# Beta inside the inverse, modulation pages of four k-tiles, edge fill through two page pools, and paired attention scores in a two-layer hybrid backbone

## The chip, the cores and the metric

The kernel runs on one core of one Trainium2 chip. The metric is device time in microseconds (us) of one execution, the median of several. The engines are TensorE (PE; its weight loads are PEld), VectorE (DVE), ScalarE (ACT), GpSimd (POOL) and SyncE (SP), whose queue issues the loads from HBM.

## The reference

Two layers over 256 latent tokens `x` and 256 context tokens, width 1024. Each layer modulates a normed stream with shift, scale and gate from `silu(c)`, runs three mixers and one output projection, and then a gated FFN with a width-3 convolution over positions.

```python
mod_l = split(silu(c) @ ada_w[layer] + ada_b[layer], 6)      # and mod_c from silu(c_ctx)
p = split_cols(modulate(rms_norm(x, g0), mod[0], mod[1]) @ w_in[layer])
# A, differential attention (4 heads): s = q k^T / 8; p = softmax(s)
w = p[:, :, 0] - lam * p[:, :, 1];  o = w @ v                 # rms_norm after it
# B, bidirectional gated linear recurrence (4 heads); it is not changed
# C, gated delta rule (4 heads, chunks of 64, both directions):
tri = eye(c) + where(strict, beta[:, None] * (k @ k.T) * decay, 0)
rhs = concat([v * beta, k * (beta * exp(gc))])
u, w = triangular_solve(tri, rhs)
v_new = u - w @ state
out = (q * exp(gc)) @ state + ((q @ k.T) * decay) @ v_new
state = exp(g_last) * state + (k * exp(g_last - gc)).T @ v_new
x = x + mod[2] * rms_norm(concat(A, B, C) @ w_out[layer], g1)
u = conv3(modulate(rms_norm(x, g2), mod[3], mod[4]) @ w_up) + b
x = x + mod[5] * rms_norm((silu(u_gate) * u_val) @ w_down, g3)
```

## The kernel before

Everything is held transposed: 128 channels on the partitions, the 512 tokens (context, then latent) along the free dimension, so the width of 1024 is eight tiles ("k-tiles"). A dense product splits weight and activation into a rounded part and a remainder and multiplies three pairs (`whi` by high, `wlo` by high, `whi` by low: lines 283 to 285, and 293 to 295 for 512 columns). Weights come as pages of 128x1024 into a ring `raw` (line 260, issued by SP), are rounded on ACT (line 269), and their remainder is taken on DVE or POOL (line 273).

In time: opening and first projections to about 100 us; mixers of layer 0 to about 400; output projection, residual, norm and the first FFN tiles to about 511 (the "layer-0 edge"); FFN of layer 0 to 810; the edge between the layers; mixers of layer 1 from about 912 to 1142; output projection and edge to 1195; FFN of layer 1 to 1345; the end.

Inside a stage, `weave` (line 1067) runs Python generators, each a stream of work (input projections, delta rule `gdn`, recurrence `hgrn`, attention `da`, modulation `ada`), and always takes the next step of the one that has progressed least, weighed by the numbers of `RATE`. A scheduler then orders the instructions for each engine, so an engine's queue differs from the order of the code. Queues run in order: what waits holds what is behind it.

*Modulation.* `ada` (line 309) makes one block of 512 columns of `silu(c) @ ada_w`. Four pages hold two k-tiles of 512 columns each; eight matmuls (line 317) with a 32-column weight, of which two columns are used, add into four groups of 32 partitions, DVE copies the bank to `adas` (line 320), four transposes turn it (line 323), and a DVE reduction (line 325) adds the four groups. Twelve blocks are made in the mixers' weaves (`ADA`), eight more as `fill` beside the edges (`FILL`: six after the mixers of layer 0, two after those of layer 1). Fill pages come from the pool `kq` (two buffers). The opening has its own `ada_unit` (line 330), whose pages hold four k-tiles of 256 columns (line 337), and whose groups are added by matmuls with the two-column constant `sel` (line 343).

*Delta rule.* `gdn` handles two halves (`hf`) of the tokens, two head pairs (`hp`) each. It forms the strictly triangular `N`, with beta multiplied in on POOL (line 658), and inverts it in six levels of doubling blocks: PE multiplies `N` by the inverse so far (`rt`), DVE masks the result (line 704), ACT and DVE transpose, PE multiplies again (`dT`), and DVE subtracts it from the inverse (line 721; line 707 at level 0). Then POOL forms `R` = beta times v (line 727, tile `gF`) and the decayed keys (line 729), and four chunk steps follow.

*Attention.* For each head and query tile `da` (line 1023) makes two score blocks (line 1035), takes their maxima, scales these by -1/8 (line 1039), exponentiates on ACT, scales the first block by its reciprocal sum (line 1047), combines the two (line 1048), and transposes the result (line 1052).

A matmul of 32-bit floats leaves two records in the trace; the dense ones and the transposes leave one.

## Time and profile before

| | |
|---|---|
| median of 3 runs | 1396.82 us (1396.49 to 1397.12) |
| the profiled execution | 1397.04 us, span 1395.3 |
| PE busy | 1298.6 us, 93% |
| PEld busy | 1048.0 us, 75% |
| DVE busy | 892.5 us, 64% |
| ACT busy | 658.9 us, 47% |
| POOL busy | 393.7 us, 28% |

The span is the time from first to last instruction of the profiled execution. A share of busy time is a mean over stages that differ. What a stage could give is read from its own windows and from the waits of the engine that ends it. Matmuls are pipelined, so the duration of a short one overlaps the next; start to start is then the better measure.

### The profile page before, as it was taken

How to read it: one execution, taken by the hardware profiler on the slowest of the kernel's cores; microseconds unless marked ns; L12 is line 12 of the kernel's file. 1: busy time of each engine (PE TensorE's matmuls, PEld its weight loads, DVE VectorE, ACT ScalarE, POOL GpSimd, SP SyncE). 2: the span in 40 equal slices, each digit the busy share in tenths (PEclk: the TensorE clock that was granted, in tenths of full speed). 3: DMA queues.
4: the chain of work that ended last, by engine and by line, in shares of the span. 5: the costliest groups of instructions: out<-in, count | busy, mean ns of one | idle time of the engine just before them, and what ended most of it. 6: DMA issues, size and time to landing. Idle time of an engine off the chain costs nothing.

```text
span 1395.3 us, 26653 instructions
## 1 busy us (share of the span) xinstructions
PE 1298.6 (93%) x10720; PEld 1048.0 (75%) x10720; DVE 892.5 (64%) x1722; ACT 658.9 (47%) x1189; POOL 393.7 (28%) x378
## 2 busy tenths in 40 slices
PE   5999997999989999999999997999989998999996
PEld 2768665666677678888888886997666765999995
DVE  3565657877647876434543559877697665776665
ACT  3364424444465544323432455675253354655553
POOL 1012014201046223201210266221241024655553
PEclk8999998999999999999999999999999999999998
DMA  8612443112335663323233234544221265455552
GB/s 300 211 46 91 167 165 139 32 47 76 107 121 189 207 217 115 104 92 105 91 101 96 82 122 135 173 145 155 95 103 34 106 243 181 139 183 185 189 167 76
DMA packets 56283, 185.96 MB, mean 133 GB/s; under 512 B 6368, under 2 KB 10464, under 8 KB 56160
## 3 DMA queue, kind: packets, MB, share of 16 engines
q1 hardware_dynamic: 56160, 184.27, 39.9%
q8 instruction: 84, 1.38, 0.4%
q14 instruction: 39, 0.32, 0.1%
HBM read 182.14 MB, written 2.10 MB: 132 GB/s over the span
## 4 chain that ended last, share of the span: by engine, by line
PE 74%; DVE 12%; ACT 5%; POOL 4%; issue 2%; DMA 2%; SPq 0%; DVEq 0%; POOLq 0%; ACTq 0%
PE up L284 8%; PE up L283 8%; PE up L285 8%; PE in L293 6%; PE in L294 5%; PE in L295 5%; PE dn L285 4%; PE dn L284 4%; PE dn L283 4%; PE ada L317 2%; DVE wlo L273 2%; PE sc L1035 2%; PE op L284 1%; PE op L283 1%; PE op L285 1%
## 5 line engine op out<-in xcount | busy, mean ns | idle before, releaser
L273 DVE TENSOR_TENSOR wlo<-raw,whi 128x1024 fp32r<-128x1024 f32 (+2 forms) x241 | 299.8, 1245 | 269.1 <-issue 90.4
L269 ACT CAST whi<-raw 128x1024 fp32r<-128x1024 f32 (+1 forms) x244 | 248.9, 1023 | 122.6 <-PE dn L285 99.0
L285 PE MATMUL up<-h,whi 128*128 128x256 f32 (+1 forms) x768 | 248.7, 324 | 1.3 <-DVE h L441 0.7
L283 PE MATMUL up<-h,whi 128*128 128x256 f32 (+1 forms) x768 | 248.3, 324 | 1.2 <-ACT h L438 1.1
L284 PE MATMUL up<-h,wlo 128*128 128x256 f32 (+1 forms) x768 | 248.0, 324 | 0.9 <-DVE wlo L273 0.9
L293 PE MATMUL in<-h,whi 128*128 128x512 f32 (+1 forms) x496 | 184.8, 373 | 2.2 <-DVE kq L481 2.2
L273 POOL TENSOR_TENSOR wlo<-raw,whi 128x256 fp32r<-128x256 f32 (+1 forms) x111 | 127.1, 1145 | 173.2 <-ACT whi L269 76.4
L294 PE MATMUL in<-h,wlo 128*128 128x512 f32 (+1 forms) x496 | 175.5, 354 | 0.0
L295 PE MATMUL in<-h,whi 128*128 128x512 f32 (+1 forms) x496 | 175.3, 354 | 0.0
L283 PEld LDWEIGHTS up<-h,whi 128*128 128x128 f32 x768 | 145.8, 190 | 19.6 <-issue 4.2
L285 PEld LDWEIGHTS up<-h,whi 128*128 128x128 f32 x768 | 145.9, 190 | 16.4 <-issue 1.7
L284 PEld LDWEIGHTS up<-h,wlo 128*128 128x128 f32 x768 | 145.9, 190 | 15.5 <-DVE wlo L273 1.9
L284 PE MATMUL dn<-gT,wlo 128*128 128x256 f32 (+1 forms) x400 | 127.6, 320 | 3.4 <-DVE wlo L273 3.4
L283 PE MATMUL dn<-gT,whi 128*128 128x256 f32 (+1 forms) x400 | 127.7, 320 | 2.7 <-ACT gT L300 2.7
L285 PE MATMUL dn<-gT,whi 128*128 128x256 f32 (+1 forms) x400 | 127.3, 320 | 0.5 <-POOL gT L302 0.5
L1262 POOL TENSOR_TENSOR u<-u 128x512 f32<-128x512 f32 (+1 forms) x44 | 44.4, 1010 | 278.3 <-DVE u L481 257.5
L293 PEld LDWEIGHTS in<-h,whi 128*128 128x128 f32 x496 | 96.2, 194 | 19.8 <-issue 5.4
L294 PEld LDWEIGHTS in<-h,wlo 128*128 128x128 f32 x496 | 96.2, 194 | 12.7 <-issue 3.5
L295 PEld LDWEIGHTS in<-h,whi 128*128 128x128 f32 x496 | 95.9, 193 | 12.3 <-issue 1.3
L477 ACT ACTIVATE u<-up,vec 128x256 f32<-128x256 f32 (+1 forms) x96 | 61.8, 644 | 75.2 <-PE up L285 75.2
L284 PEld LDWEIGHTS dn<-gT,wlo 128*128 128x128 f32 x400 | 76.7, 192 | 9.1 <-DVE wlo L273 4.0
L283 PEld LDWEIGHTS dn<-gT,whi 128*128 128x128 f32 x400 | 76.8, 192 | 8.2 <-ACT gT L300 3.1
(281 smaller groups left out, 2318.2 us busy)
## 6 DMA issues: line engine op xcount, KB each, us to landing
raw<-ada_w SPq DMA_DIRECT2D x96, 512.0 KB, 4.4
raw<-w_up SPq DMA_DIRECT2D x96, 512.0 KB, 3.5
raw<-w_in SPq DMA_DIRECT2D x68, 512.0 KB, 3.6
raw<-w_down SPq DMA_DIRECT2D x32, 512.0 KB, 3.5
raw<-w_out SPq DMA_DIRECT2D x24, 512.0 KB, 3.5
raw<-w_down SPq DMA_DIRECT2D x24, 384.0 KB, 3.1
x<-xT SPq DMA_DIRECT2D x16, 256.0 KB, 6.1
x_spill<-x SPq DMA_DIRECT2D x8, 128.0 KB, 2.0
```

What stands on the lines that cost most here:

```text
L269: nc.scalar.copy(hi[:, :cols], raw[:, :cols])
L273: e.tensor_sub(lo[:, a:b], raw[:, a:b], hi[:, a:b].bitcast(F32))
L283: nc.tensor.matmul(ps, wh[:, k, :], ah, start=first and k == ks[0], stop=False)
L284: nc.tensor.matmul(ps, wl[:, k, :], ah, start=False, stop=False)
L285: nc.tensor.matmul(ps, wh[:, k, :], al, start=False, stop=last and k == ks[-1])
L293: nc.tensor.matmul(ps, wh[:, k, :], ah, start=k == 0, stop=False)
L294: nc.tensor.matmul(ps, wl[:, k, :], ah, start=False, stop=False)
L295: nc.tensor.matmul(ps, wh[:, k, :], al, start=False, stop=k == n - 1)
L317: nc.tensor.matmul(ps[32 * g:32 * g + 32, :], self.cs[:, k, :], w[:, kk, :], start=k < 4, stop=k >= 4, tile_position=(0, 32 * g))
L477: nc.scalar.activation(dst, ps, AF.Identity, scale=w3[1], bias=bias)
L1035: nc.tensor.matmul(ps[:, :128 * nk], q[64 * m:64 * m + 64, a + 128 * qt:a + 128 * qt + 128], k[64 * m:64 * m + 64, :128 * nk], start=True, ...
L1262: self.nc.gpsimd.tensor_mul(us[0][:, lo:], us[0][:, lo:], us[1][:, lo:])
```

## The change

*Modulation pages.* A page now holds four k-tiles of 256 columns; a block is sixteen matmuls in two column halves, chained so that the scheduler keeps their order. Four `sel` matmuls take the place of the transposes and of the reduction. Fill pages are taken from `g` and `kq` in turn; `g` has six buffers, not seven, and the delta rule no longer takes a page for `R`.

*Delta rule.* Beta is folded into the inverse: the inverse starts from beta on the diagonal, `N` carries only a sign, and at level 0 it is multiplied by beta of one token and, transposed, of the other. The masks go: DVE's subtraction becomes a predicated copy that writes only the positions of this level, and ACT copies `rt` out of PSUM. `R` is the plain value, copied by ACT.

*Attention.* The 1/8 is applied as ACT moves q and k out of PSUM; the maximum is negated as it is taken; both score blocks of a query tile are issued as a pair; the scaling of the first block goes to ACT.

```diff
-RATE = ((121, 197, 32, 218, 37, 8), (53, 64, 15, 50, 5, 7))
+RATE = ((118, 137, 32, 147, 37, 8), (53, 64, 15, 65, 5, 7))
...
@@ ada
-            for kc in range(4):
-                w = self.load_raw(self.I["ada_w"][12 * ly + j - 4, kc], 1024, tags[kc % len(tags)]).rearrange("p (k n) -> p k n", k=2)
...
+            prev = []
+            for i in range(4):
+                half, kc = i // 2, i % 2
+                w = self.load_raw(self.I["ada_w"][12 * ly + j - 4, i], 1024, tags[i % len(tags)]).rearrange("p (k n) -> p k n", k=4)
+                for g in range(4):
+                    x = nc.tensor.matmul(ps[32 * g:32 * g + 32, 256 * half:256 * half + 256], self.cs[:, 4 * kc + g, :], w[:, g, :],
+                                         start=kc == 0, stop=kc == 1, tile_position=(0, 32 * g))
+                    prev = [self._dep(x, prev)]
...
-                nc.tensor.transpose(ps2[:, 128 * i:128 * i + 128], st[:, i * 128:(i + 1) * 128], self.C("ident"))
-            sm = self.small("adr", 8)
-            nc.vector.reduce_sum(sm, ps2.rearrange("p (a g s) -> p a s g", a=4, g=4)[:, :, 0:2, :], axis=AX.X)
+                nc.tensor.matmul(ps2[:, 2 * i:2 * i + 2], st[:, 128 * i:128 * i + 128], self.C("sel"), start=True, stop=True)
...
@@ gdn
-                nc.gpsimd.tensor_tensor(ck(X[hp]), ck(X[hp]), b64(hp, "beta"), ALU.mult)
...
-                nc.vector.tensor_tensor(ck(N[hp]), ck(N[hp]), pkv[hp][:, :, 0, :], ALU.mult)
+                nc.vector.scalar_tensor_tensor(ck(N[hp]), ck(N[hp]), -1.0, pkv[hp][:, :, 0, :], ALU.mult, ALU.mult)
...
-                nc.scalar.copy(ck(MT[hp]), self.C("i64").unsqueeze(1).to_broadcast([P, 8, 64]))
+                nc.gpsimd.tensor_tensor(ck(MT[hp]), self.C("i64").unsqueeze(1).to_broadcast([P, 8, 64]), b64(hp, "beta"), ALU.mult)
...
+                def fill(t, src):
...
+                    nc.vector.copy_predicated(out, m.bitcast(U32), v(src))
...
-                        nc.vector.transpose(mtx[hp], N[hp])
-                for hp in HP:
-                    nc.vector.tensor_tensor(ck(rt[hp]), ck(src[hp]), hgm[:, lev, :].unsqueeze(1).to_broadcast([P, 4, 64]), ALU.mult)
+                        b4 = lambda n: G[n][:, 8 * hp + 4 * hf:8 * hp + 4 * hf + 4].unsqueeze(2).to_broadcast([P, 4, 64])
+                        nc.vector.tensor_tensor(ck(rt[hp]), ck(N[hp]), b4("bo"), ALU.mult)
+                        nc.vector.transpose(mtx[hp], rt[hp])
+                        nc.vector.tensor_tensor(ck(mtx[hp]), ck(mtx[hp]), b4("bi"), ALU.mult)
...
+                for hp in HP:
+                    nc.scalar.copy(rt[hp], src[hp])
...
-                    nc.vector.tensor_tensor(joint(MT[hp], 0, 4, 0), joint(MT[hp], 0, 4, 0), nb(ps2[hp][:, 0:256]), ALU.subtract)
+                    fill(MT[hp], ps2[hp][:, 0:256])
...
-                nc.gpsimd.tensor_tensor(s4(R[hp]), two(vtok[hp]), bsc(hp, "beta"), ALU.mult)
+                nc.scalar.copy(vb[hp], tok[hp][:, 256:512])
...
@@ da
+                    qs = (qt,)
+                    ps = [self.bank("a", "sc") for m in range(2)]
...
+                        for m in (1, 0):
...
-                    nc.vector.tensor_scalar(mx, mx, -0.125, None, ALU.mult)
...
+                        nc.vector.reduce_max(mx[m][:, :len(qs)], ps[m][:, :128 * nk], axis=AX.X, negate=True)
...
-                nc.vector.tensor_scalar(e[0], e[0], rc[0], None, ALU.mult)
...
+                nc.scalar.activation(e0, e0, AF.Copy, scale=r0)
...
@@ mixers
-        self.fill = self.ada_gen([(l, j) for l in range(DEPTH) for j in FILL[ly][l]], "g", ("kq",))
+        self.fill = self.ada_gen([(l, j) for l in range(DEPTH) for j in FILL[ly][l]], "g", ("g", "kq"))
```

How this moves instructions, at three places.

SP's queue at the layer-1 edge, before: `raw` pages are loaded from the output projection's, the modulation's and the FFN's weights. The four loads 11969 to 11981 are those of the last modulation block.

```order
L260 DMA raw_11899<-ada_w 128x1024
L260 DMA raw_12029<-w_up 128x1024
L260 DMA raw_12064<-w_up 128x1024
L260 DMA raw_12106<-w_up 128x1024
L260 DMA raw_12141<-w_up 128x1024
L260 DMA raw_12181<-w_up 128x1024
L260 DMA raw_12216<-w_up 128x1024
L260 DMA raw_11969<-ada_w 128x1024
L260 DMA raw_11973<-ada_w 128x1024
L260 DMA raw_11977<-ada_w 128x1024
L260 DMA raw_11981<-ada_w 128x1024
L260 DMA raw_12257<-w_up 128x1024
```

The same place after. The modulation pages 12078 and 12090 (pool `g`) and 12084 and 12096 (pool `kq`) are those of the last block.

```order
L261 DMA raw_12002<-ada_w 128x1024
L261 DMA raw_12008<-ada_w 128x1024
L261 DMA raw_12078<-ada_w 128x1024
L261 DMA raw_12090<-ada_w 128x1024
L261 DMA raw_12144<-w_up 128x1024
L261 DMA raw_12179<-w_up 128x1024
L261 DMA raw_12221<-w_up 128x1024
L261 DMA raw_12256<-w_up 128x1024
L261 DMA raw_12296<-w_up 128x1024
L261 DMA raw_12331<-w_up 128x1024
L261 DMA raw_12084<-ada_w 128x1024
L261 DMA raw_12096<-ada_w 128x1024
```

Two of the last block's four loads have moved ahead of the six `w_up` loads; the other two still stand behind them.

PE's queue at the same edge, before: `ada_11968` is the bank of the last modulation block, `up` are the first FFN matmuls.

```order
L317 MATMUL ada_11968<-raw_11973,cs 32x512 x2
L283 MATMUL up_12036<-h_11576,whi_12031 128x256
L284 MATMUL up_12036<-h_11576,wlo_12032 128x256
L283 MATMUL up_12071<-h_11576,whi_12066 128x256
L284 MATMUL up_12071<-h_11576,wlo_12067 128x256
L283 MATMUL up_12113<-h_11576,whi_12108 128x256
L285 MATMUL up_12036<-h_11576,whi_12031 128x256
L285 MATMUL up_12071<-h_11576,whi_12066 128x256
L317 MATMUL ada_11968<-raw_11977,cs 32x512 x2
L317 MATMUL ada_11968<-raw_11981,cs 32x512 x2
L323 MATMUL ada_2062_11987<-consts,adas_11985 128x128 x4
L283 MATMUL up_12036<-h_11577,whi_12031 128x256
```

The same place after, with `ada_12077` as the last block; `ss` are the column sums of the norm.

```order
L318 MATMUL ada_12077<-raw_12090,cs 32x256
L383 MATMUL ss_12045<-sq_12053,consts 128x256
L383 MATMUL ss_12045<-sq_12056,consts 128x256
L383 MATMUL ss_12045<-sq_12059,consts 128x256
L383 MATMUL ss_12045<-sq_12062,consts 128x256
L383 MATMUL ss_12045<-sq_12065,consts 128x256
L318 MATMUL ada_12077<-raw_12090,cs 32x256 x3
L318 MATMUL ada_12077<-raw_12096,cs 32x256 x4
L284 MATMUL up_12151<-h_11679,whi_12146 128x256
L285 MATMUL up_12151<-h_11679,wlo_12147 128x256
L325 MATMUL ada_2080_12104<-consts,adas_12102 128x2 x4
L284 MATMUL up_12186<-h_11679,whi_12181 128x256
```

The last two page pieces of the block stood behind seven `up` matmuls and now stand in front of the first; the matmuls that add the groups stand behind two.

POOL's queue in the second half of the delta rule of layer 0, before: `gA` (line 658) is the decay times beta, `gF` (line 727) is `R`, `gB` the decayed keys.

```order
L678 COPY sgl_2152<-gB_1985 128x8
L678 COPY sgl_2153<-gB_1986 128x8
L658 TENSOR_TENSOR gA_1983<-gA_1983,sbeta_640 128x512
L727 TENSOR_TENSOR gF_2725<-gB_1985,sbeta_640 128x512
L729 TENSOR_TENSOR gB_1985<-gB_1985,skd_676 128x256
L727 TENSOR_TENSOR gF_2725<-gB_1986,sbeta_640 128x512
L729 TENSOR_TENSOR gB_1985<-gB_1985,skd_676 128x256
L729 TENSOR_TENSOR gB_1986<-gB_1986,skd_676 128x256 x2
L658 TENSOR_TENSOR gA_1984<-gA_1984,sbeta_640 128x512
```

The same place after; `gC` is the start of the inverse.

```order
L685 COPY sgl_2486<-gB_2274 128x8
L687 TENSOR_TENSOR gC_2488<-consts,sbeta_640 128x512
L687 TENSOR_TENSOR gC_2489<-consts,sbeta_640 128x512
L685 COPY sgl_2487<-gB_2275 128x8
L748 TENSOR_TENSOR gB_2274<-gB_2274,skd_676 128x256 x2
L748 TENSOR_TENSOR gB_2275<-gB_2275,skd_676 128x256 x2
```

The multiplications into `gA` and `gF` are gone; two of the same size from a constant have come.

## Rows read from the trace of the kernel before

**Rows 1.** Windows: length, busy us (records) of each engine, granted clock, DMA share, GB/s.

```profile
100.00:400.00 300.00, 276.61 (x3065) 196.37 (x3063) 200.18 (x491) 134.25 (x301) 55.61 (x53) 0.96 0.29 99
207.40:234.10 26.70, 18.38 (x218) 12.25 (x218) 22.24 (x49) 11.03 (x22) 15.59 (x12) 0.92 0.51 178
230.00:244.00 14.00, 10.53 (x119) 7.24 (x121) 9.69 (x34) 9.54 (x21) 0.00 (x0) 0.51 0.13 39
400.00:525.00 125.00, 116.62 (x819) 95.19 (x820) 88.27 (x144) 67.31 (x121) 49.31 (x47) 0.98 0.60 199
950.00:1150.00 200.00, 185.98 (x2344) 133.35 (x2344) 146.75 (x384) 91.18 (x196) 41.38 (x36) 0.97 0.35 122
1038.00:1046.00 8.00, 6.10 (x56) 5.38 (x58) 6.30 (x16) 2.69 (x5) 0.74 (x1) 0.57 0.67 243
1200.00:1345.00 145.00, 145.00 (x1210) 145.00 (x1210) 97.61 (x135) 81.17 (x122) 79.17 (x86) 1.00 0.58 183
```

**Rows 2.** PE's waits from 100 to 400: waiter, releaser, total us, times, longest.

```profile
PE rt L602 <- DVE gC L707: 8.3, 1, 8.3
PE wt L1052 <- DVE em L1048: 5.0, 6, 1.3
```

**Rows 3.** PE's waits from 950 to 1150.

```profile
PE wt L1052 <- DVE em L1048: 6.6, 5, 2.8
PE ada L323 <- DVE adas L320: 2.8, 1, 2.8
```

**Rows 4.** PE's waits from 400 to 525.

```profile
PE ada L317 <- DMA raw<-ada_w: 2.3, 3, 0.9
```

**Rows 5.** Windows of line 317 (modulation matmuls) alone: length, PE (records), PEld, clock.

```profile
100.00:400.00 300.00, 14.71 (x112) 2.95 (x112) 0.96 0.29 99
400.00:525.00 125.00, 20.09 (x80) 2.83 (x80) 0.98 0.60 199
```

**Rows 6.** Timeline of PE: start, us, engine, line, operation, tiles, shape, count.

```profile
54.29 1.07 PE L337 MATMUL ada<-raw,cs 128*32 128x256 f32 x16
...
56.11 0.50 PE L343 MATMUL ada<-consts,adas 128*128 128x2 f32 x4
56.47 0.47 PE L283 MATMUL in<-h,whi 128*128 128x512 f32 x1
...
468.58 0.60 PE L323 MATMUL ada<-consts,adas 128*128 128x128 f32 x4
468.94 0.36 PE L284 MATMUL up<-h,wlo 128*128 128x256 f32 x1
```

**Rows 7.** Timeline at the layer-1 edge, SP's queue and PE (in brackets: idle before, releaser).

```profile
1168.21 10.82 SPq L260 DMA_DIRECT2D raw<-ada_w  x4
...
1180.00 0.40 PE L285 MATMUL up<-h,whi 128*128 128x256 f32 x2
1181.92 3.16 PE L317 MATMUL ada<-raw,cs 128*32 128x512 f32 x8 [1.52 <-DMA raw<-ada_w]
...
1186.62 0.39 PE L283 MATMUL up<-h,whi 128*128 128x256 f32 x1
```

**Rows 8.** Timeline of POOL and DVE around 220 us.

```profile
215.56 3.70 POOL L727 TENSOR_TENSOR gF<-gB,sbeta 128x512 f32<-128x512 f32 x1
...
226.82 1.72 DVE L668 TENSOR_TENSOR gA<-gA 128x256 f32<-128x256 f32 x1 [3.18 <-POOL gA L658]
```

**Rows 9.** Groups: line, engine, operation, tiles, shapes, count; busy us, mean ns; idle before, releaser.

```profile
L704 DVE TENSOR_TENSOR rt<-rt,consts 128x256 f32<-128x256 f32 x40 | 15.1, 410 | 6.2 <-PE rt L602 6.2
...
L917 DVE COPY_PREDICATED Stot<-consts,hs 128x128 f32<-128x128 uint32 (+1 forms) x36 | 13.6, 438 | 1.6 <-PE hs L892 1.6
...
L1047 DVE TENSOR_SCALAR em<-em,ssm 128x512 f32<-128x512 f32 (+1 forms) x24 | 10.5, 436 | 0.4
...
L710 ACT COPY gC<-gC 128x256 f32<-128x256 f32 x20 | 8.2, 410 | 21.5 <-DVE gC L721 15.3 <-DVE mod L326 4.5 <-DVE gC L707 1.1
...
L1039 DVE TENSOR_SCALAR smx<-smx 128x1 f32<-128x1 f32 x48 | 6.9, 145 | 0.4
```

More of the change, by code (lines that the diff above doesn't have):

```diff
@@ L80 @@
 _n = 0
-for _name, _w in (("ident", 128), ("ones", 128), ("sel", 2), ("sel8", 16), ("eps", 1), ("one", 1), ("bones", 128),
+for _name, _w in (("ident", 128), ("ones", 128), ("sel", 2), ("par", 2), ("sel8", 16), ("eps", 1), ("one", 1), ("bones", 128),
                   ("obones", 128), ("perm", 128), ("i64", 64), ("inc2", 128), ("ninc2", 128), ("pstr2", 128),
@@ L311, in ada @@
             ps = self.bank(bank, "ada")
-            for kc in range(4):
-                w = self.load_raw(self.I["ada_w"][12 * ly + j - 4, kc], 1024, tags[kc % len(tags)]).rearrange("p (k n) -> p k n", k=2)
-                for kk in range(2):
-                    k = 2 * kc + kk
-                    g = k % 4
-                    nc.tensor.matmul(ps[32 * g:32 * g + 32, :], self.cs[:, k, :], w[:, kk, :], start=k < 4, stop=k >= 4,
-                                     tile_position=(0, 32 * g))
+            prev = []
[6 more added lines that the diff above has]
+                    prev = [self._dep(x, prev)]
             st = self.tmp("d2", "adas")
@@ L486, in proj_copy, with evac @@
         yield from self.dense_gen(ps[:, lo:], w, hT, lo, NTOK)
-        self.evac(idx, dst[:, lo:], ps[:, lo:])
+        self.evac(idx, dst[:, lo:], ps[:, lo:], 0.125 if idx >= DA_Q else None)
         yield
-    def evac(self, idx, dst, src):
-        if idx % 2:
+    def evac(self, idx, dst, src, scale=None):
+        if scale is not None:
+            self.nc.scalar.activation(dst, src, AF.Copy, scale=scale)
+        elif idx % 2:
             self.nc.scalar.copy(dst, src)
@@ L753, in gdn @@
                     for s, j in enumerate(js):
-                        self.quad((ck(ps[hp])[H[g], s, :], MTv[hp][H[g], j, :], rv[hp][H[g], j, :], True, True) for g in range(2))
+                        self.quad((ck(ps[hp])[H[g], s, :], MTv[hp][H[g], j, :], rv[hp][s][H[g]], True, True) for g in range(2))
                     nc.scalar.copy(pair(U[hp], i), ck(ps[hp][:, 0:128]))
@@ L1031, in da @@
             for qt in range(2):
-                e, rc = [], []
-                for m in range(2):
-                    ps = self.bank("a", "sc")
-                    nc.tensor.matmul(ps[:, :128 * nk], q[64 * m:64 * m + 64, a + 128 * qt:a + 128 * qt + 128],
-                                     k[64 * m:64 * m + 64, :128 * nk], start=True, stop=True)
-                    mx = self.small("mx", 1, 4)
-                    nc.vector.reduce_max(mx, ps[:, :128 * nk], axis=AX.X)
-                    nc.vector.tensor_scalar(mx, mx, -0.125, None, ALU.mult)
-                    em = self.tmp("d2", "em")[:, :128 * nk]
-                    sm = self.small("sm", 1, 4)
-                    self.act(em, ps[:, :128 * nk], AF.Exp, scale=0.125, bias=mx, accum_out=sm)
-                    nc.vector.reciprocal(sm, sm)
-                    e.append(em)
-                    rc.append(sm)
```

65 lines of the change are left out of this document (49 added, 16 removed).

## The prediction

> **What bounds the kernel now.** I read the page first, then TensorE's waits stage by stage, then the stages as windows, then one place in each. In the page PE is busy 1298.6 us of a 1395.3 us span, and the chain that ended last is PE for 74%: TensorE's queue sets the end, and a gain must come off PE's busy time, its idle time or its clock. The windows say where there is room [rows 1]. From 1200 to 1345 us PE is busy all 145 us with 1210 matmul records at clock 1.00, 0.12 us a record: nothing that other engines do matters there. The layer-0 mixers (100 to 400) leave PE idle 23.4 us, the first layer-0 edge (400 to 525) 8.4, the layer-1 mixers (950 to 1150) 14.0. In two short stretches the granted clock reads 0.51 and 0.57, near the lower of its two levels (1.2 GHz against 2.4), behind stalls. The waits name the releasers: in the layer-0 mixers one wait of 8.3 us in front of the inverse's first matmuls, ended by VectorE's level-0 subtraction, and 5.0 us for VectorE's `em` [rows 2]; in the layer-1 mixers 6.6 us for `em` and one of 2.8 us for `adas` [rows 3]; at the layer-0 edge 2.3 us for modulation pages [rows 4].
>
> **The sum** is made against the profiled execution, 1397.04 us (span 1395.3 and 1.7 around it), 0.2 us above the median of the runs shown, so the result compares with the median without correction.
>
> *Modulation pages.* A page goes from two 512-column matmuls to four of 256 in four column groups. Old pages at the layer-0 edge stand alone between dense matmuls: 80 records, 20 pages, take 20.09 us, 1.00 a page; in the layer-0 mixers, where the four pages of a block run together, 112 records, 28 pages, take 14.71 us, 0.53 a page [rows 5]. Two pages of the new form, which the opening's `ada_unit` already uses, take 1.07 us, 0.535 each [rows 6]. So the new form is worth 0.47 a page at the edges and nothing in the mixers.
>
> *Column sums by matmul.* Four transposes take 0.36 us start to start; two of the two-column `sel` matmuls also 0.36, so the four now needed take 0.72, +0.36 a block [rows 6]. The VectorE reduction that goes is off TensorE's path. Bounds: 0 a block if these records overlap their neighbours when four stand together, +0.36 if not; I take +0.36, a measured row of the same instruction. The Trainium skill (TensorEngine Tiling (Array Packing), Instruction Overhead) speaks the other way: a matmul costs about 60 cycles however few its columns. An estimate from that page: eight passes a block, 60 cycles each at 2.4 GHz, 0.20 us, 0.16 less than the transposes, and the sum below would come to about 1370. The trace disagrees, with 0.36 us for four such passes, and I go by the trace.
>
> *Layer-0 edge.* Five blocks: 20.09 falls to 20 x 0.535 = 10.7, and `sel` adds 5 x 0.36 = 1.8: 7.6 us less on PE. Of it 2.3 us was page waiting, which I let go with it, since fill pages now come from two pools instead of one. VectorE is busy 88.27 of these 125 us [rows 1] and its norm chain ends part of PE's idle time, so some is given back: bounds -8.5 and +1, I take **-5.0**, nearer the full saving.
>
> *Layer-1 edge.* Four page loads occupy the head of SP's queue from 1168.21 for 10.82 us. PE's last `up` pair ends at 1180.40; the next dense matmul starts at 1186.62; between them stand two pages, with 1.52 us waited for a load, then the copy and transposes [rows 7]. Of 6.2 us only 1.07 + 0.36 is work: 4.8 lost. By the order the last block's pages now stand in front of the first `up` matmuls, no longer behind seven of them, and two of its four pages go to buffers that need not wait for the block before. What is late next is the pair of page loads behind six `w_up` loads; they are queued on SP, and nothing but later `w_up` waits behind them. The four other pages there save 4 x 0.47, less 2 x 0.36 for `sel`, 1.2, half of it counted: -0.6. Together **-5.4**; bounds -7 (all) and +5.5 (the two pages land as late again as the gap now).
>
> *Mixers, modulation.* 112 records are 7 blocks; layer 1 holds about as many (6.5): 13.5 x 0.36 = **+4.9**, nothing for pages. Bounds 0 and +6.
>
> *Inverse.* On VectorE all 48 mask multiplications go (40 at 410 ns, in all 15.1 us, and the eight of level 0, which turn into one of the two new multiplications a unit). The subtraction of each level becomes a predicated copy: no row has its shape; the nearest has 438 ns as a mean of a larger and a smaller one against 410 for arithmetic of this shape [rows 9]. Between 0.29 and 0.73 I take 0.44, 48 x 0.03 = +1.4. Level 0 gets 16 multiplications for its eight masks, eight more: 8 x 0.41 = +3.3. ScalarE takes 40 copies of 410 ns into the mask's place, one after the other, so a level's chain is as long as before: the gain is room on VectorE, not a shorter chain. On POOL two multiplications by beta go and one by beta on an identity comes, off the path. There a real wait ends: the subtraction at 226.82 waited 3.18 us for POOL's `gA`, which stood behind two `gF`, the first 3.70 us long [rows 8]; both are gone from in front (POOL's order above). From 207.4 to 234.1 VectorE is busy 22.24 of 26.7 us [rows 1], so the rest of the 8.3 is its own chain, which the change doesn't shorten. Of the 3.18 come off two of the added multiplications, 0.8, and 0.6 for PE's filler, which by the order is some five matmuls of 0.12 us shorter there: I take **-1.8** of the 8.3; bounds 0 and -8.3.
>
> *Attention.* 48 sign-and-scale instructions (6.9 us) and 24 scalings of `em` (10.5 us) leave VectorE; the 24 go to ScalarE beside its 134 busy of 300 and 91 of 200 [rows 1, 9]. On the chain behind `em` a unit loses 2 x 0.145, and the scaling runs beside a reciprocal and a product on VectorE. With VectorE some 28 us lighter in both layers (15.1 + 6.9 + 10.5 - 1.4 - 3.3), I let half of the `em` waits go: **-2.5** in layer 0, **-3.3** in layer 1; bounds 0 and all. Paired scores move matmuls past each other, none goes: 0. The `adas` wait in layer 1 is a copy late in a busy VectorE: -2 of 2.8.
>
> *Clock.* The stretch from 230 to 244 has 10.53 us of PE work at 0.51, that from 1038 to 1046 6.10 at 0.57 [rows 1]; at the upper level they would be 5.4 and 3.5. The first stands right behind the 8.3 stall. If the stall is shorter some of it goes: **-3.0** and **-1.7**; bounds 0 and -5.1, -2.6.
>
> *Tail of layer 0.* The rates are set anew, and by the order the last of the delta rule's matmuls stand among the first output projections: 20 fewer dense matmuls lie ahead as cover, 20 x 0.12 = **+2.4**. The smaller page pool, the constants, the smaller scratch: 0; no wait for a page of `g` is in the rows, and if it came its cover would be the same weave.
>
> Layer 0 mixers -1.8 - 2.5 - 3.0 = -7.3; layer 1 mixers -3.3 - 2 - 1.7 = -7.0. The sum: -5.0 - 5.4 + 4.9 - 7.3 - 7.0 + 2.4 = -17.4, so **1379.6 us**.
>
> **Rivals.**
> *The stalls go wholly.* A lighter VectorE and POOL would empty the waits [rows 2, 3] and keep the clock up. What I left of them: 6.5 + 2.5 + 2.1 in layer 0, 3.3 + 0.8 + 0.9 in layer 1, 16.1 together: 1363. For it: the 8.3 wait is one place, the clock hangs on it. Against: VectorE is busy 200 of 300 us, and the chain there is longer than its filler.
>
> *Given back in the mixers.* Every level now goes from PE to ScalarE, PE and VectorE in turn, and `em` from ScalarE to VectorE by way of ScalarE again; if each handover costs what the removed instruction did, both mixers' 14.3 us stay: 1394. For it: the chain is no shorter by count. Against: the POOL wait is truly gone.
>
> *Slower: bundled pages.* At the edges a block's sixteen matmuls now stand as one piece in PE's in-order queue. If one of its pages lands late, dense matmuls behind it wait, where before a single page was interleaved. The price is that of the gap above, 4.8, with the waiting copy behind it some 5.5 us (6.2 less 0.7 for the copy and transposes that stay), times eight fill blocks, 44 at most; from the point where four of the eight pay it, the sum (-17.4 + 22) is above zero; with five paying, 1407. For it: fill loads are queued behind `w_up` loads. Against: page waits at the layer-0 edge are only 2.3 us [rows 4], and two pools hold twice the pages.
>
> **How the numbers follow.** What a measurement of this kernel can tell from no change is about 0.2%, 2.8 us. Forecast 0.52, own range 1370 to 1388. Stalls wholly gone 0.18. Given back 0.18, half of it within 0.2%. Bundled pages 0.12. Faster 0.52 + 0.18 + 0.09 = 0.79, same 0.09, slower 0.12. The range, 1358 to 1398, holds the first three with their bounds and leaves out the slow rival and the far end of the fast one.
>
> **What would show it.** In the new profile: fill pages at 1.07 a pair, near 11 us of them at the layer-0 edge; the `sel` matmuls at 0.72 a block; the gap at 1180 to 1186 down to its 1.4 us of work; no wait of VectorE on POOL before `gA`'s sums, and the wait for `gC` near 6.5; `em` waits at about half in both layers. The forecast is wrong if PE waits for `ada_w` more than 5 us at the edges, or if a new wait for a ScalarE copy inside the inverse is as large as the ones that went.

## The result, and the profile after

The changed kernel takes 1381.09 us (median of 4 runs, 1374.31 to 1383.56) against 1396.65 before; the ratio is 0.9895, 95% interval 0.9866 to 0.9924. The forecast was 1379.6. The profiled execution took 1379.79 us (span 1378.0), 17.25 less than that of before. The sum came out; several of its terms did not, and that is what follows. One program's executions differ by up to 14 us (experiment 1), so the nearness is partly chance.

The windows of both kernels, cut at the same events (last gate projection, first output projection, first FFN product, first down projection, and in layer 1 last gate projection to first output projection, first FFN product to last down projection); columns as in [rows 1]. First before:

```profile
77.80:359.90 282.10, 263.98 (x2809) 188.18 (x2808) 188.30 (x449) 130.96 (x278) 51.56 (x46) 0.96 0.29 96
359.90:453.20 93.30, 83.82 (x744) 69.05 (x744) 57.68 (x125) 48.38 (x109) 38.66 (x38) 0.95 0.44 149
453.20:582.10 128.90, 124.03 (x714) 97.61 (x713) 87.31 (x131) 62.76 (x96) 32.45 (x29) 1.00 0.51 166
582.10:856.60 274.50, 266.89 (x1307) 225.86 (x1305) 136.40 (x162) 103.50 (x141) 66.14 (x59) 1.00 0.32 102
897.70:1140.70 243.00, 229.28 (x2735) 174.16 (x2734) 184.07 (x461) 123.78 (x253) 45.57 (x41) 0.98 0.35 121
1179.30:1382.70 203.40, 197.77 (x1597) 193.01 (x1598) 134.99 (x198) 110.26 (x169) 105.71 (x115) 0.98 0.51 161
```

The same six stretches after:

```profile
76.30:362.70 286.40, 268.98 (x3009) 196.24 (x3008) 184.60 (x418) 147.17 (x324) 43.35 (x42) 0.97 0.29 94
362.70:440.70 78.00, 73.53 (x703) 65.07 (x704) 48.91 (x89) 48.14 (x105) 38.71 (x38) 0.98 0.61 206
440.70:561.40 120.70, 116.10 (x794) 100.45 (x793) 84.30 (x123) 61.57 (x94) 32.88 (x28) 1.00 0.49 162
561.40:840.20 278.80, 270.66 (x1307) 229.63 (x1305) 136.88 (x163) 103.70 (x141) 65.28 (x59) 0.98 0.32 101
881.10:1128.60 247.50, 231.95 (x2849) 180.69 (x2848) 179.43 (x418) 134.10 (x282) 40.26 (x37) 0.97 0.36 118
1167.00:1365.40 198.40, 195.96 (x1593) 194.51 (x1594) 131.64 (x197) 109.42 (x169) 108.82 (x116) 0.98 0.51 160
```

The reader is to see: the mixers of layer 0 grew by 4.3 us, the output projection fell by 15.3, the first FFN tiles by 8.2; the down projection, whose code is not touched, grew by 4.3; the mixers of layer 1 grew by 4.5 where 4.6 less was forecast (7.0 gained, some 2.4 lost to the column sums); layer 1's FFN with its edge fell by 5.0. The whole gain is in the edges.

The clock column warns that one profile doesn't settle a stretch. In the down projection PE stands still 3.0 us for `wlo` in both kernels (waits from 560 to 860, before and after; total, times, longest), but only after does the clock fall behind it.

```profile
PE dn L284 <- DVE wlo L273: 3.4, 2, 3.0
```

```profile
PE dn L285 <- DVE wlo L274: 3.0, 1, 3.0
```

So the next table takes the half clock out: from each stretch, half of the time in which PE was busy at the lower level (worked out from the unrounded records; from the rows above it is about PE busy times one minus PEclk). It is an estimate, since it takes PE's work at the upper level to need half the time. Its stretches end a matmul or two away from those above, which shifts a value by up to 0.4 us. "Again" is the changed kernel profiled a second time (experiment 1); the others are experiments below, by number.

| stretch | before | after | again | 2 old modulation | 3 old inverse | 4 old attention | 5 old rates | 6 rates alone | 7 transposes |
|---|---|---|---|---|---|---|---|---|---|
| mixers, layer 0 | 273.6 | 277.9 | 278.6 | 278.1 | 274.5 | 277.8 | 274.3 | 273.2 | 273.7 |
| output projection 0 | 88.8 | 76.4 | 74.8 | 75.0 | 76.5 | 79.3 | 88.9 | 80.3 | 75.4 |
| first FFN tiles 0 | 128.7 | 120.5 | 120.4 | 128.5 | 120.5 | 120.5 | 120.5 | 128.2 | 119.7 |
| down projection 0 | 274.3 | 273.9 | 274.0 | 273.2 | 273.9 | 276.0 | 274.2 | 273.9 | 274.3 |
| mixers, layer 1 | 238.8 | 241.0 | 242.1 | 237.8 | 237.5 | 241.3 | 239.2 | 238.4 | 238.5 |
| output projection 1 | 38.6 | 38.4 | 38.7 | 41.9 | 38.5 | 37.6 | 39.1 | 38.8 | 39.3 |
| FFN 1 | 200.1 | 194.8 | 194.6 | 199.4 | 197.3 | 195.4 | 197.3 | 201.0 | 196.4 |

The down projection, whose code is the same everywhere, is now 273 to 274 but for 276 with the old attention, which speaks for the estimate, and the second profile agrees with the first within 1.6 us a line. What the change did: +4 to +5 in the mixers of layer 0, -12 to -14 in the output projection, -8 in the first FFN tiles, +2 to +3 in the mixers of layer 1, -5 in FFN 1.

Waits of PE after, from 100 to 400 and then from 950 to 1150, answering to [rows 2, 3]:

```profile
PE rt L610 <- DVE gC L704: 4.5, 4, 1.5
PE wt L1081 <- DVE em L1077: 3.2, 4, 1.2
PE ada L325 <- DVE adas L322: 2.1, 3, 1.7
```

```profile
PE wt L1081 <- DVE em L1077: 3.6, 3, 1.6
PE rt L610 <- DVE gC L704: 2.7, 2, 1.5
```

The 8.3 us in one piece have become 4.5 in four, the waits for `em` went from 5.0 to 3.2 and from 6.6 to 3.6, and the one for `adas` in layer 1 is gone while 2.1 us for it came in layer 0.

### The profile page after: what moved, and what is told of

It reads as the page before. It is cut to its first block, busy times and chain, and to the rows that moved or that the text cites. A ratio compares the mean times of both kernels' runs of the same rounds, so it can differ in the third digit from the quotient of the medians.

```text
span 1378.0 us, 27368 instructions
## 1 busy us (share of the span) xinstructions
PE 1288.8 (94%) x11120; PEld 1067.5 (77%) x11120; DVE 870.2 (63%) x1600; ACT 683.8 (50%) x1257; POOL 382.9 (28%) x370
## 4 chain that ended last, share of the span: by engine, by line
PE 76%; DVE 12%; ACT 4%; POOL 3%; issue 2%; DMA 2%; SPq 0%; DVEq 0%; POOLq 0%; ACTq 0%
PE up L284 8%; PE up L285 8%; PE up L286 8%; PE in L294 6%; PE in L295 5%; PE in L296 5%; PE dn L286 4%; PE dn L285 4%; PE dn L284 4%; DVE wlo L274 2%; PE sc L1059 2%; PE ada L318 2%; PE op L286 1%; PE op L284 1%; PE op L285 1%
## 5 line engine op out<-in xcount | busy, mean ns | idle before, releaser
L274 DVE TENSOR_TENSOR wlo<-raw,whi 128x1024 fp32r<-128x1024 f32 (+2 forms) x241 | 295.4, 1227 | 256.1 <-PE up L285 90.9
L286 PE MATMUL dn<-gT,whi 128*128 128x256 f32 (+1 forms) x400 | 128.5, 322 | 0.7 <-POOL gT L303 0.7
L1291 POOL TENSOR_TENSOR u<-u 128x512 f32<-128x512 f32 (+1 forms) x44 | 49.1, 1117 | 277.9 <-DVE u L481 271.1
L951 POOL TENSOR_TENSOR K<-K,F 128x512 f32<-128x512 f32 x24 | 36.0, 1501 | 189.0 <-ACT kj L932 167.0
```

The lines of the kernel that those rows point to most:

```text
L274: e.tensor_sub(lo[:, a:b], raw[:, a:b], hi[:, a:b].bitcast(F32))
L286: nc.tensor.matmul(ps, wh[:, k, :], al, start=False, stop=last and k == ks[-1])
L951: nc.gpsimd.tensor_tensor(joint(K2, a, a + NTOK), joint(K2, a, a + NTOK), tot(a, a + NTOK, False), ALU.mult)
L1291: self.nc.gpsimd.tensor_mul(us[0][:, lo:], us[0][:, lo:], us[1][:, lo:])
```

## The experiments

Each ran in five rounds against the kernel before on the same chip. The text compares experiments by these ratios: a difference to the changed kernel (0.9904) times 1395 us. Each ratio is uncertain by 2 to 4 us, so a difference by some 5.

**1. The changed kernel again.** No edit.

> The changed kernel once more, unchanged. Four executions of it lay between 1374.3 and 1383.6 us, with mean clocks of 0.980 to 0.970 that fall as the time rises. Theory 'clock': the instructions and waits repeat, and only the places differ at which the granted clock falls behind a wait, so the times spread over some 8 us again and in the new profile some half-clock stretches are at other places than 216.7, 247.4, 817.5 and 943.8 us. In particular the fall in the down projection (817.5, 6.8 us), which the kernel before did not have behind the same wait of 3.0 us, need not be there; without it the stage from the first down projection's end to the third's is about 231 us, not 235. Theory 'fixed': the falls are the order's doing, the same places show, 235 again.

1381.16 us (1372.45 to 1386.44), ratio 0.9904 [0.9873, 0.9935]. Mean clocks run from 0.979 at the fastest to 0.969 at the slowest, a spread of 14 us with one program; 17 runs of the kernel before in the same job lay between 1390.53 and 1400.2. Its profile, the down projection of layer 0 and the mixers of layer 1:

```profile
560.00:838.60 278.60, 270.44 (x1309) 229.57 (x1308) 136.65 (x164) 104.17 (x143) 65.98 (x59) 0.98 0.33 101
879.40:1121.20 241.80, 225.86 (x2849) 175.87 (x2848) 178.75 (x418) 133.76 (x282) 40.24 (x37) 1.00 0.37 120
```

The mixers of layer 1 take 241.8 us at clock 1.00, where the first profile had 247.5 at 0.97, with the same matmuls: 5.7 us that lie with the clock. So 'clock' holds there. It missed the down projection: 278.6 again, with the lower clock behind the same wait. That this stage needs no fall shows in the kernel before and in experiment 7, 274.5 and 274.6 us at clock 1.00 with the same wait of 3.0 us. Which executions fall at which wait stays open.

**2. Old modulation.**

```diff
-            for i in range(4):
-                half, kc = i // 2, i % 2
+            for kc in range(4):
...
-                nc.tensor.matmul(ps2[:, 2 * i:2 * i + 2], st[:, 128 * i:128 * i + 128], self.C("sel"), start=True, stop=True)
+                nc.tensor.transpose(ps2[:, 128 * i:128 * i + 128], st[:, i * 128:(i + 1) * 128], self.C("ident"))
...
-        self.fill = self.ada_gen([(l, j) for l in range(DEPTH) for j in FILL[ly][l]], "g", ("g", "kq"))
+        self.fill = self.ada_gen([(l, j) for l in range(DEPTH) for j in FILL[ly][l]], "g", ("kq",))
```

> The changed kernel with the old modulation blocks: two k-tiles a page, eight 512-column matmuls, four transposes and a reduction, fill pages from one pool. Theory 'terms' (each part is worth its own term of the sum: edges -5.0 and -5.4, mixers +4.9): 5.5 us slower than the changed kernel, 1386 to 1387; PE's occupancy by modulation up at the layer-0 edge by some 8 us and down in the mixers by some 4. Theory 'fit' (the rates and the order are set for the whole, and any part undone throws the weave out of step): 10 us or more slower. Rival 'nothing': the layer-0 edge is bound by VectorE, within 2 us.

1383.96 us, 0.9909 [0.9881, 0.9937]: 0.7 us slower than the changed kernel, not told from nothing, though the medians are 2.8 apart. By the number this is the rival 'nothing', but not by its reason. The table shows why: the first FFN tiles return to 128.5 and both stages of the layer-1 edge lose 3.2 and 4.8, but the mixers of layer 1 are 3 to 4 us shorter. With the clock out the profile is 10 to 11 us longer than the two of the changed kernel. 'Terms' has the places right; the clock, 0.975 to 0.982 here, gives the rest back.

**3. Old inverse.**

```diff
-                    fill(MT[hp], ps2[hp][:, 0:256])
+                    nc.vector.tensor_tensor(joint(MT[hp], 0, 4, 0), joint(MT[hp], 0, 4, 0), nb(ps2[hp][:, 0:256]), ALU.subtract)
...
-                    nc.scalar.copy(rt[hp], src[hp])
+                    nc.vector.tensor_tensor(ck(rt[hp]), ck(src[hp]), hgm[:, lev, :].unsqueeze(1).to_broadcast([P, 4, 64]), ALU.mult)
...
+                nc.gpsimd.tensor_tensor(ck(X[hp]), ck(X[hp]), b64(hp, "beta"), ALU.mult)
...
+                nc.gpsimd.tensor_tensor(s4(R[hp]), two(vtok[hp]), bsc(hp, "beta"), ALU.mult)
```

> The changed kernel with the old inverse: beta on POOL, masks and subtractions on VectorE, R on POOL. Theory 'terms': 4.8 us slower (the 1.8 of the stall and the 3.0 of its clock), 1385 to 1386, with one long wait of PE for the level-0 result in the second half of layer 0. Theory 'fit': 10 us or more slower. Rival 'given back': the handover from PE to ScalarE inside each level costs what the mask did, within 2 us, and layer 1 alone, where the stall before was 0.9 us, gets faster by 2 to 4.

The edit also gives the pool `g` its seventh page back and the delta rule its page for `R`, which the excerpt leaves out.

1375.57 us, 0.985 [0.9823, 0.9876]: 7.5 us faster (5.6 by the medians). Both theories fall; 'given back' is short of it. Both mixers are 3 to 5 us shorter. Groups of instructions (columns as in [rows 9]); first the changed kernel:

```profile
L704 DVE COPY_PREDICATED gC<-consts,dT 128x256 f32<-128x256 uint32 x40 | 18.1, 502 | 21.0 <-PE dT L610 20.8
...
L748 POOL TENSOR_TENSOR gB<-gB,skd 128x256 f32<-128x256 f32 x16 | 14.4, 905 | 36.0 <-ACT svb L746 35.4
...
L704 DVE COPY_PREDICATED gC<-consts,gC 128x256 f32<-128x256 uint32 x8 | 10.2, 1465 | 0.0
...
L720 DVE TENSOR_TENSOR gC<-gC,sbi 128x256 f32<-128x256 f32 x8 | 4.9, 637 | 0.0
```

Then this one:

```profile
L722 DVE TENSOR_TENSOR gC<-gC,dT 128x256 f32<-128x256 f32 x40 | 15.3, 414 | 14.1 <-PE dT L603 13.9
L705 DVE TENSOR_TENSOR rt<-rt,consts 128x256 f32<-128x256 f32 x40 | 15.2, 413 | 5.4 <-PE rt L603 5.2
...
L730 POOL TENSOR_TENSOR gB<-gB,skd 128x256 f32<-128x256 f32 x16 | 12.7, 796 | 1.0
...
L708 DVE TENSOR_TENSOR gC<-gC,rt 128x256 f32<-128x256 f32 x8 | 5.6, 741 | 0.0
```

The predicated copy takes 502 ns on average where the subtraction took 414, and at level 0 1465 where it took 741. These means hide the pattern. The changed kernel's copies by source line 704, as least, median and largest ns:

```profile
L704 DVE COPY_PREDICATED gC<-consts,dT x40: 432/448/774, 146.1 to 1063.0; 128x256 f32<-128x256 uint32 x40
...
L704 DVE COPY_PREDICATED gC<-consts,gC x8: 1248/1408/1958, 127.2 to 1025.9; 128x256 f32<-128x256 uint32 x8
```

The pieces that a level writes double in length from level to level. At level 0 (single elements) a copy takes 1248 ns or more, at level 1 (pairs) all eight take 704 to 774, and from level 2 on (pieces of four and more) all 32 take 432 to 455. One copy of level 1 and two of level 2:

```profile
939.67 0.73 DVE L704 COPY_PREDICATED gC<-consts,dT 128x256 f32<-128x256 uint32 x1
...
950.72 0.78 DVE L704 COPY_PREDICATED gC<-consts,dT 128x256 f32<-128x256 uint32 x2 [1.07 <-PE dT L610]
```

The subtractions take 403 to 425 ns at all levels from 1 on. Two other means are lifted by single long instructions: the 741 (median 632, one of 1510) and the 637 of the multiplication by the second beta (median 399, two near 1370).

In all, the new inverse left VectorE no room: it is busy 870.2 us in the changed kernel and 868.6 here. What grew is level 0. In the first half of layer 1, the changed kernel and then this one (the transposes between are alike):

```profile
928.13 0.72 DVE L720 TENSOR_TENSOR gC<-gC,sbi 128x256 f32<-128x256 f32 x2
928.77 2.48 DVE L704 COPY_PREDICATED gC<-consts,gC 128x256 f32<-128x256 uint32 x2
```

```profile
923.48 0.71 DVE L705 TENSOR_TENSOR rt<-gC,consts 128x256 f32<-128x256 f32 x2
924.12 1.11 DVE L708 TENSOR_TENSOR gC<-gC,rt 128x256 f32<-128x256 f32 x2
```

From its first instruction (a multiplication by the first beta there, a transpose here) level 0 takes 4.5 us there and 2.4 here. PE's waits for the inverse, over the whole execution, there and here:

```profile
PE rt L610 <- DVE gC L704: 8.9, 7, 1.7
```

```profile
PE rt L603 <- DVE gC L722: 3.7, 3, 1.6
...
PE rt L603 <- DVE gC L708: 1.3, 1, 1.3
```

These are 8.9 us and 5.0. The one long wait that 'terms' expected did not come: with the old inverse the longest for level 0 is 1.3 us. POOL's decayed keys wait 35.4 us in all for ScalarE's copy of v in the changed kernel, where POOL's idle time before them is 1.0 here; that this costs PE anything isn't shown.

**4. Old attention.**

```diff
-                        nc.vector.reduce_max(mx[m][:, :len(qs)], ps[m][:, :128 * nk], axis=AX.X, negate=True)
+                    nc.vector.tensor_scalar(mx, mx, -0.125, None, ALU.mult)
...
-                nc.scalar.activation(e0, e0, AF.Copy, scale=r0)
+                nc.vector.tensor_scalar(e[0], e[0], rc[0], None, ALU.mult)
```

> The changed kernel with the old attention: scores one by one, 1/8 in the exponent, 48 scalings of the maximum and 24 of the first block on VectorE. Theory 'terms': the waits for the combined block come back to 5.0 and 6.6 us, with the modulation wait and its clock about 9 us slower, 1390. Theory 'fit': more than 12. Rival 'nothing': other work fills PE's queue while it waits, within 2 us.

1388.54 us, 0.9949 [0.9929, 0.9968]: 6.3 us slower (7.4 by the medians). The size is near 'terms', the path isn't: the waits for `em` did not return (2.2 and 3.8 us), and with the clock out the output projection of layer 0 is 3 to 4 us longer, the down projection 2, the mixers no more than before the edit. In all the profile is then 3 to 5 us longer; the rest is a lower clock.

**5. Old rates.**

```diff
-RATE = ((118, 137, 32, 147, 37, 8), (53, 64, 15, 65, 5, 7))
+RATE = ((121, 197, 32, 218, 37, 8), (53, 64, 15, 50, 5, 7))
```

> The changed kernel with the old rates. The profiles so far, with the time lost to the half clock taken out, put the change's gain at the layer-0 edge (output projection 88.8 to 76.4 us, first FFN tiles 128.7 to 120.5) and a loss in the mixers of layer 0 (273.6 to 277.9); with the old modulation the output projection stays at 75.0 and only the FFN tiles return to 128.5. Theory 'rates' (the new rates pull the ends of the mixers ahead of the output projection): with the old rates the output projection is at 86 to 89 again, the mixers some 4 us shorter, the whole 6 to 10 us slower than the changed kernel. Theory 'terms' (the prediction): 2.4 us faster. Rival 'room': it is the lighter VectorE that shortened that stage, within 2 us.

1389.44 us, 0.9968 [0.995, 0.9986]: 8.9 us slower; 'terms' is refuted. The output projection stands at 88.9 again, with everything else new, and the mixers of layer 0 are 3.6 to 4.3 us shorter, as 'rates' said.

**6. New rates alone.** The same edit the other way round, in the kernel before.

> The kernel before with the new rates alone. Theory 'rates': the output projection's stage falls from 88.8 to about 77 and the mixers of layer 0 grow by 4, 6 to 9 us faster than before. Theory 'terms': 2.4 us slower. Rival 'fit' (the rates only suit the new streams): slower by more than 3 us.

1385.32 us, 0.9945 [0.9925, 0.9965] against the kernel before: 7.7 us faster. So the rates are worth 8 to 9 us with old and new streams alike. Two details of 'rates' missed: the output projection fell to 80.3, not 77, and the mixers of layer 0 did not grow (273.2). In the changed kernel undoing the rates, the inverse or the column sums each takes some 4 us from these mixers, so their growth is not the rates' alone. The waits for `em` fell here too, with the old attention (from 100 to 400, then from 950 to 1150):

```profile
PE wt L1052 <- DVE em L1048: 3.9, 5, 2.3
```

```profile
PE wt L1052 <- DVE em L1048: 3.7, 3, 2.7
```

The stretch from the first output-projection matmul to where these run on undisturbed; before, after, and here:

```profile
359.90:397.90 38.00, 32.34 (x370) 22.33 (x369) 23.82 (x78) 17.10 (x49) 4.34 (x7) 0.95 0.32 112
```

```profile
362.70:389.00 26.30, 25.26 (x297) 19.61 (x297) 17.13 (x41) 16.65 (x46) 7.30 (x9) 0.94 0.55 191
```

```profile
352.50:384.10 31.60, 29.11 (x288) 20.17 (x288) 18.78 (x49) 16.65 (x45) 7.61 (x9) 0.91 0.38 130
```

38.0 us have become 26.3 and 31.6. In it the last recurrence and attention steps run in short chains with little dense work left to lie between them: PE is idle 5.7 us of 38.0 before, 1.0 of 26.3 after and 2.5 of 31.6 here; the rest of the difference is work that now lies elsewhere (370 matmul records before, 297 and 288 with the new rates). With the new rates the attention and the delta rule yield to the recurrence earlier on, whose last 64 state updates (`hu`) then stand before that stretch instead of in it.

**7. Transposes on the new pages.**

```diff
-                nc.tensor.matmul(ps2[:, 2 * i:2 * i + 2], st[:, 128 * i:128 * i + 128], self.C("sel"), start=True, stop=True)
+                nc.tensor.transpose(ps2[:, 128 * i:128 * i + 128], st[:, i * 128:(i + 1) * 128], self.C("ident"))
+            sm = self.small("adr", 8)
+            nc.vector.reduce_sum(sm, ps2.rearrange("p (a g s) -> p a s g", a=4, g=4)[:, :, 0:2, :], axis=AX.X)
```

> The changed kernel with its new pages, but the four groups added by four transposes and a VectorE reduction as before, in place of the four two-column matmuls. Theory 'terms': the two-column matmuls cost 0.36 us a block more, twenty blocks, so this is 7 us faster where all blocks lie on PE's path, 4 to 7 with cover, and the mixers of layer 1 are 2 to 3 us shorter. Rival 'short': a narrow matmul is cheaper than a wide transpose, so 3 us slower. Rival 'nothing': within 2 us.

1369.77 us, 0.9839 [0.9813, 0.9864]: 9.1 us faster (11.3 by the medians). The groups of the changed kernel, and of this one:

```profile
L325 PE MATMUL ada<-consts,adas 128*128 128x2 f32 x160 | 21.7, 258 | 3.8 <-DVE adas L322 3.6
...
L325 PEld LDWEIGHTS ada<-consts,adas 128*128 128x128 f32 x160 | 21.4, 205 | 6.5 <-DVE adas L322 5.8
```

```profile
L325 PE MATMUL ada<-consts,adas 128*128 128x128 f32 x80 | 13.2, 291 | 2.9 <-DVE adas L322 2.7
...
L325 PEld LDWEIGHTS ada<-consts,adas 128*128 128x128 f32 x80 | 9.6, 148 | 5.5 <-DVE adas L322 4.7 <-issue 0.2
```

160 records of 258 ns against 80 of 291, and as many weight loads of 205 ns against 148: 8.5 us of PE time by the first pair. Start to start a record costs about the same, 0.10 us for the two-column one (eight in 0.81, below) and 0.09 for the transpose (four in 0.36, [rows 6]), and there are twice as many: the two columns save nothing. With the clock out this profile is 4 to 6 us shorter than the two of the changed kernel; the rest of the 9.1 is the clock.

**8. Old inverse, old pages and transposes in the mixers.** The edit of experiment 3, and:

```diff
-            self.ada(ly, [j], tags, bank)
+            (self.ada if tags != ("raw",) else self.ada_old)(ly, [j], tags, bank)
```

> The changed kernel with the old inverse (1375.6 us by itself) and, for the twelve modulation blocks made in the mixers, the old pages, transposes and reduction; the eight fill blocks keep the new form and both page pools. Theory 'parts add': the old inverse gives 5.6 us, and the mixers of layer 1 another 3 to 4 (clock taken out, they were 237.8 with the old pages against 241 to 242), layer 0 nothing: 1371 to 1373. Theory 'terms': 4.9 faster than the old inverse by itself, 1371. Rival 'fit': another order in the weave takes it back, 1375 to 1380.

1363.18 us, 0.979 [0.9765, 0.9816]: 30 us less than before, 18 less than the changed kernel by the medians; faster than 'parts add'.

**9. Old inverse, and transposes on all new pages.** The edits of experiments 3 and 7.

> The changed kernel with the old inverse and, on all new pages, transposes and a reduction in place of the two-column matmuls: both edits that made the changed kernel faster, together. Theory 'parts add': 1381.1 less 5.6 (old inverse) less 11.3 (transposes) is 1364; against the version with old pages in the mixers (1363.2) the same, since there only the eight fill blocks differ: 8 x 0.4 less at the edges, 3 us faster, and new pages in the mixers' place. So 1360 to 1365. Rival 'fit': the weave takes it back, 1367 to 1372.

1363.3 us, 0.9761 [0.9744, 0.9777]: the parts add. Experiments 8 and 9 beat both kernels, and neither is told from the other: their medians are equal, their ratios 4 us apart on two chips.

**10. Masks with beta inside.**

```diff
-                    nc.scalar.copy(rt[hp], src[hp])
+                    nc.vector.tensor_tensor(ck(rt[hp]), ck(src[hp]), hgm[:, lev, :].unsqueeze(1).to_broadcast([P, 4, 64]), ALU.mult)
...
-                    fill(MT[hp], ps2[hp][:, 0:256])
+                    nc.vector.tensor_tensor(joint(MT[hp], 0, 4, 0), joint(MT[hp], 0, 4, 0), nb(ps2[hp][:, 0:256]), ALU.add)
```

> The changed kernel with beta inside the inverse as changed, but masks and additions as before: VectorE masks rt (410 ns) where ScalarE copies it, and adds into the inverse (414 ns, 741 at level 0) where the predicated copy writes (502 ns, 1465 at level 0). Theory 'copy' (the predicated copy's price is what the new inverse costs): half or more of the 5.6 us come back, 1375 to 1378. Theory 'fold' (the extra multiplications at level 0, and the decayed keys that wait for the copy of v, cost it): 1380 to 1384. Rival 'load': VectorE's 40 more masks slow the attention, 1384 to 1388.

1377.53 us, 0.9867 [0.985, 0.9884]: 5.2 us faster (3.6 by the medians), where 'copy' put it, at the edge of what these intervals tell. Taking back the predicated copies, with 48 masks more on VectorE and still six pages in `g`, gives half or more of what experiment 3 gave, so the seventh page is not needed for that part. PE's waits for the inverse lie between:

```profile
PE rt L610 <- DVE gC L740: 3.5, 4, 1.5
PE rt L610 <- DVE gC L724: 3.4, 2, 2.4
```

That is 6.9 us, against 8.9 with the predicated copies and 5.0 with the old inverse. VectorE is busy 880.2 us here, 10 more than in the changed kernel, and this costs nothing that shows.

**11. The copy of rt on VectorE.**

```diff
-                    nc.scalar.copy(rt[hp], src[hp])
+                    nc.vector.tensor_copy(rt[hp], src[hp])
```

> The changed kernel with the copy of rt out of PSUM on VectorE in place of ScalarE, 40 copies of about 0.4 us; everything else as changed. Theory 'handover' (ScalarE's queue in the middle of each level costs the time): faster by 3 to 6 us, 1375 to 1378. Theory 'copy' (the price sits in the predicated copies on VectorE): slower by 2 to 6 us, since VectorE takes on 16 us, 1383 to 1387. Rival 'nothing': within 2 us.

1381.22 us, 0.9896 [0.9875, 0.9916]: the same. 'Handover' falls, and 'copy' as worded here too: 40 copies more on VectorE (880.1 us busy) cost nothing that can be told.

**12. One page pool for the fill.**

```diff
-        self.fill = self.ada_gen([(l, j) for l in range(DEPTH) for j in FILL[ly][l]], "g", ("g", "kq"))
+        self.fill = self.ada_gen([(l, j) for l in range(DEPTH) for j in FILL[ly][l]], "g", ("kq",))
```

> The changed kernel with fill pages from one pool (two buffers) again. Theory 'terms': the second pool is what keeps page loads ahead; without it PE waits for pages at both edges, 4 to 8 us slower, with more than 3 us of page waits in the layer-1 edge. Rival 'pages' (the shorter page form alone makes the gain, and two buffers are enough): within 2 us. Rival 'stall': each of the eight sixteen-matmul pieces waits for its last two pages, 15 us or more slower.

1393.41 us, 0.9993 [0.9973, 1.0013]: 12.4 us slower, the whole gain of the change. PE's waits at the layer-1 edge, here and in the changed kernel:

```profile
PE ada L318 <- DMA raw<-ada_w: 3.8, 3, 1.7
```

```profile
PE ada L318 <- DMA raw<-ada_w: 1.0, 3, 0.6
```

'Terms' has the sign and the place, not the size. With the clock out the profile is 7.3 us longer than the changed kernel's, all of it at the edges: first FFN tiles 3.1, the two stages of the layer-1 edge 2.4 and 1.9, output projection of layer 0 1.2. Its mean clock was 0.962 to 0.974 over twelve runs. How much of the rest is the order and how much the clock stays open.

## Why the prediction was right, and where it wasn't

The time was right within 1.5 us, and the likeliest case's own range held it; that it came so near is luck, because two terms failed by about as much in opposite ways. By its steps:

- *Pages at the edges* (-5.0 and -5.4): right in place and mechanism, the first too small. With the clock out the first FFN tiles fell by 8.2, the full saving, so nothing was given back to VectorE's norm chain as I had allowed; FFN 1 fell by 5.3. PE waits 1.0 us for `ada_w` at the layer-1 edge, far from the 5 that would have refuted the forecast. The new pages cost what I read from the opening, 0.54 each: 192 records, 24 pages, in 13.04 us, in line 318's own window (columns as in [rows 5]):

```profile
384.00:485.00 101.00, 13.04 (x192) 5.75 (x192) 1.00 0.65 218
```

  At the layer-1 edge the gap of 6.2 us closed as forecast. PE's timeline there:

```profile
1164.90 1.06 PE L318 MATMUL ada<-raw,cs 128*32 128x256 f32 x14
1167.05 0.39 PE L284 MATMUL up<-h,whi 128*128 128x256 f32 x1 [1.08 <-ACT h L438]
...
1167.39 0.95 PE L325 MATMUL ada<-consts,adas 128*128 128x2 f32 x8
1168.20 0.36 PE L284 MATMUL up<-h,whi 128*128 128x256 f32 x1
```

  The pages are done before the first `up`, the column sums stand behind two.
- *Column sums* (+0.36 a block): right in sign, somewhat low. Here eight records take 0.81 us start to start; experiment 7 puts the twenty blocks at 9.1 us, 0.46 a block with the clock's part in it. The Trainium skill (TensorEngine Tiling (Array Packing), Instruction Overhead) gives a fixed overhead of about 60 cycles for each matmul; by the prediction's estimate from it these would have been 0.16 cheaper a block. This kernel shows 0.45 more.
- *Inverse with its clock* (-1.8 and -3.0): wrong. Experiment 3: +7.5. Two steps failed. The first is one price for all predicated copies, 0.44 us: it holds from level 2 on (0.43 to 0.46), but level 1 measured 0.70 to 0.77 and level 0 1.465, twice my upper bound. So 28.3 us of predicated copies stand against 20.9 of subtractions, 7.4 more where +1.4 was forecast. The second is "a level's chain is as long as before: the gain is room on VectorE": level 0 of the chain became longer (4.5 us for 2.4 in the first half of layer 1), there was no room (870.2 us busy against 868.6 with the old inverse), and room was not what counted, for experiments 10 and 11 took 10 us of it at no cost. PE's waits for the inverse are 8.9 us in all, where the kernel before had 9.2, and 2.6 with the new rates. How the loss divides between the predicated copies and the two multiplications by beta at level 0 stays open: experiment 10 gives the copies half or more, within its uncertainty. ScalarE's copy of `rt` is not the cause: PE waits 1.2 us in all for it, and experiment 11 moved it at no gain.
- *POOL's wait* at `gA` is gone as forecast, but the 8.3 us stall is no proof for it: with the new rates alone the stall is gone too, and PE's longest wait for the inverse there is 1.7 us. It is gone as well with the old inverse under the new rates (experiment 3).
- *Attention* (-2.5, -3.3, with the `adas` wait and the clock of layer 1 some -9.5): sign right, 6.3; the way isn't shown to be the `em` waits, which the new rates alone brought to 3.9 and 3.7 and the old attention did not bring back.
- *Tail of layer 0* (+2.4): wrong, -8 to -9. I read one stream from the order, the delta rule, and did not ask what moved out of the tail: the recurrence's updates. In the trace the delta rule does end later, its last matmul at 352 us instead of 316, but still 10 us before the first output projection at 363.
- *The second page pool* stood in the reasons for the edges and had no term of its own; experiment 12 puts 12 us on it, 7 with the clock out.

So the sum was right because the rates were 11 us better than forecast and the inverse 12 us worse. The parts undone singly (rates 8.9, attention 6.3, modulation 0.7, inverse -7.5) add up to 8.4 us of the 13.4 that the ratio 0.9904 gives; the rest is within their uncertainty, or the parts help each other. Of the rivals, 'given back in the mixers' has the result for the inverse, though not by its handovers (experiment 11); 'bundled pages' did not happen with two pools (page waits 1.0 us in all at the layer-1 edge), and did in part with one.

## What to carry to other kernels

Give every instruction form its own row before it is priced: a form seen only in other shapes and access patterns can cost twice the upper bound that these suggest, and a mean over levels can hide it. Before room on an engine is counted as gain, ask whether the chain gets shorter. When rates or orders change, list what enters and what leaves each stretch with little cover, for all streams. And test a change of many parts by undoing one at a time: here the pages with their second pool, the attention and the rates gained, the column sums and the inverse lost, and the version without these two is 18 us better than the whole.
